# State-space products issued alternately from both partition halves and divided into parts between the k-steps of dense units

## The chip, the cores and the metric

The kernel runs on one core of a Trainium2 chip. The metric is device time in microseconds (us) for one execution. TensorE (PE in the profile) multiplies matrices, VectorE (DVE), ScalarE (ACT) and GpSimd (POOL) do the elementwise work, and SyncE (SP) issues the DMA transfers. Each engine works through its own instruction list in order and waits on semaphores.

## The reference

One layer of a streaming encoder is computed for 1024 prompt positions (with 16 meta tokens ahead of them) and 32 decode positions. An input projection of the normalised rows yields latents for attention, the channels `u` of a state-space mixer and two gates. The state-space mixer is what the change touches:

```
bu = einsum("blgc,gnc->blgn", u, b)              # 64 groups of 16 channels, 64 complex states each
x  = f * bu                                       # complex
h  = associative_scan over positions of lam * h + x
y  = Re(einsum("blgn,gcn->blgc", h, c)) + d * u
s  = gelu(y);  o_b = (s @ w_glu_v) * sigmoid(s @ w_glu_g)
h  = h + (sigmoid(g_a) * o_a + sigmoid(g_b) * o_b) @ w_out
h  = h + relu(rmsnorm(h) @ w_mlp_up)**2 @ w_mlp_down
```

All inputs, weights and outputs are float32.

## The kernel before

All activations lie as 128 channels by 1056 or 1072 positions; a position is (k, t) with t in 0..7, so that the scan over positions is done on 134 blocks of 8 positions, and the products inside a block of 8 are one matrix `M`.

**Dense units.** Each large product is cut into units of 128 output columns. `lin_part` runs over the 8 k-steps of a unit; each k-step has three products (high and low halves of weights and activations in fp32r) times three column chunks, so nine matmuls, 72 in a unit. Their results gather in PSUM tiles `acc` (5 banks in this stage) and are copied out by `finish` on ScalarE. `Weights.get` loads the weights two units ahead and splits them into `wh` (ScalarE, L184) and `wl` (GpSimd, L187) one unit ahead.

**The state-space stage.** It covers about 60 to 470 us of the profile. Eight blocks j of 128 channels (8 groups g of 16) pass through six steps:

- `st0`: loads `U` (the channels of the block), builds the phase table `tb` on GpSimd, and the tables `cl` (tile `clm`) and `wx` (tile `wxt`) on VectorE.
- `st1`: transposes `wx` into `W` (L580), forms the kernel of a block (L590, four quarters of the array's columns), and spreads it by DMA into `M`.
- `st2`: 16 fp32 matmuls (L614) with 64 output rows each, alternately for the lower and the upper 64 columns of the array, give the inputs of the scan in tile `sp`; ScalarE copies them to `xs` (L620 to L622), and VectorE does the scan: `A`, `Bt` (L634 to L637), two scans (L640), two products (L642, L643) and `hb` (L646, L647), the states. All of it needs `tb`.
- `st3`: for each of 8 groups one fp32 matmul with `M` and 128 rows (L662), then two with `cl` and `hb` on 64 rows (L664). Even groups have their states in partitions 0 to 63, odd groups in 64 to 127. Every fp32 matmul stands in the trace as two MATMUL records. ScalarE copies the sums out (L668).
- `st4`, `st5`: GELU on ScalarE, VectorE and GpSimd.

The tiles `sp` of st1, st2 and st3 share three PSUM banks (pool `sps`). `tb`, `xs`, `hb`, `W` and some others have one buffer each, so block j+1 begins `tb` when block j no longer reads it.

**Order.** `START` places the blocks at slots 2, 4, 7, 9, 12, 15, 17 and 20; step d of block j is emitted in slot START[j]+d (st3 has d = 4), and a slot holds all steps due in it, whole, and then one dense unit. The framework turns the emission order into priorities: on each engine the first instruction in emission order that its model of time holds to be ready comes next, and the order so found is fixed before the kernel runs. So slots 6, 11 and 19 hold st3 of one block and st2 of another, slots 8, 13, 16 and 21 st3 and st1, and slot 24 st3 alone. Blocks 0, 2 and 5 are followed by the next block after two slots, the others after three.

After the stage come two more dense units, the GLU units (from about 533 us), attention, the output projections and the MLP.

Of the kernel before, what the change touches and what calls it, by code (L numbers as in the profile page):

```python
# [10 lines left out]
F32 = mybir.dt.float32  # L11
# [3 lines left out]
AF = mybir.ActivationFunctionType  # L15
# [17 lines left out]
KQ = 132  # L33
NQT = T * KQ
CH = [(0, 358), (358, 358), (716, 356)]
CQ = [(0, 352), (352, 352), (704, 352)]
# [86 lines left out]
GQ = [(t0 * KQ, nt * KQ) for t0, nt in G3]  # L123
# [34 lines left out]
def tile_layer(ctx: ExitStack, tc: tile.TileContext, a: dict, o: list, dbg=None):  # L158
    nc = tc.nc
# [77 lines left out]
    w_units = [("u", m) for m in range(8)]  # L237
# [4 lines left out]
    for kind, m in w_units:  # L242
        w0, M = (m * 128, 128 if m < 5 else 64) if kind == "z" else (NQ + 1024 * "uab".index(kind) + m * 128, 128)
# [15 lines left out]
            units += ups(q + 1, range(1, GK))  # L259
    ws = Weights(units)  # L260

    def lin_part(ps, wh, wl, xh, xl, ks, kt, M, chunks):
        for k in ks:
            for p, (w, x) in enumerate(((wh, xh), (wh, xl), (wl, xh))):
                for (c0, n), pt in zip(chunks, ps):
                    nc.tensor.matmul(  # L266
                        pt[:M, :n], lhsT=w[:, k, :], rhs=x(k, c0, n),
                        start=(k == 0 and p == 0), stop=(k == kt - 1 and p == 2),
                    )
        return [(c0, n, pt[:M, :n]) for (c0, n), pt in zip(chunks, ps)]  # L270

    def lin(pool, tag, wh, wl, xh, xl, kt, M=128, chunks=CQ):
        ps = [pool.tile([128, 512], F32, tag=tag, name=tag) for _ in chunks]
        return lin_part(ps, wh, wl, xh, xl, range(kt), kt, M, chunks)

    def rsqrt(pool, v, shape, tag, cap=None):
        R, n = shape
# [22 lines left out]
    gps = ges.enter_context(tc.tile_pool(reuse_waits="tile", name="gps", bufs=5, space=PSUM))  # L300
    with tc.tile_pool(reuse_waits="tile", name="s5", bufs=1) as sp, tc.tile_pool(reuse_waits="tile", name="sps", bufs=3, space=PSUM) as sps:
        xh = xnp.tile([128, 8, NT], F32R, name="xh")
        xl = xnp.tile([128, 8, NT], F32R, name="xl")
        xfull = [lambda k, c0, n, x=x: x[:, k, c0:c0 + n] for x in (xh, xl)]
        xout = [lambda k, c0, n, x=x: x[:, k].rearrange("p (t c) -> p t c", t=T)[:, c0 // KQ:(c0 + n) // KQ, 0:KQ]
                for x in (xh, xl)]

        def finish(kind, m, M, outs, st):
            for c0, n, ps in outs:
                if kind in "ab":  # L310
                    nc.scalar.activation(st[:M, c0:c0 + n], ps, AF.Tanh, scale=0.5)  # L311
                else:
                    nc.scalar.activation(st[:M, c0:c0 + n], ps, AF.Copy)
# [2 lines left out]

        stage = [lambda: sp.tile([128, NT], F32, tag="gst", name="gst", bufs=2)]

        def run_unit(kind, m):
            wh, wl = ws.get()  # L320
            M = 64 if (kind, m) == ("z", 5) else 128
            st = stage[0]()
            if kind == "u" or (kind == "z" and m > 2):
                finish(kind, m, M, lin(gps, "acc", wh, wl, *xfull, 8, M, CH), st)
                nc.sync.dma_start(dst_d[kind][m][:M], st[:M])
            else:
                finish(kind, m, M, lin(gps, "acc", wh, wl, *xout, 8, M, GQ), st)
# [82 lines left out]
        with ExitStack() as _:  # L410
# [102 lines left out]
            for q, nme in enumerate(("ssm_c_re", "ssm_c_im")):  # L513
                cl = sp.tile([128, 4, 2, 64], F32, tag="clt", name="cl")
# [59 lines left out]
            def st1(j):  # L574
                cl, wx = hold[j]["cl"], hold[j]["wx"]
                W = sp.tile([128, 2, 4, 128], F32, tag="W", name="W")
                for q in range(2):
                    pp = sps.tile([128, 4, 128], F32, tag="sp", name="sp")
                    for g in range(4):
                        nc.tensor.transpose(pp[:, g], wx[:, q, g].rearrange("p a b -> p (a b)"), ident)  # L580
                    nc.scalar.activation(W[:, q], pp, AF.Copy)

                for g2 in range(2):
                    hs = slice(64 * g2, 64 * g2 + 64)
                    for q in range(2):
                        V.tensor_copy(bd[hs, q, :, g2, :], bbar[hs, q, 4 * j:4 * j + 4])
                pk = sps.tile([128, 512], F32, tag="sp", name="sp")
                for g in range(4):
                    for q in range(2):
                        nc.tensor.matmul(  # L590
                            pk[32 * g:32 * g + 32, 0:128],
                            lhsT=bd[:, q, g].rearrange("p a b -> p (a b)"),
                            rhs=cl[:, q, g, 0:8].rearrange("p a b -> p (a b)"),
                            start=(q == 0), stop=(q == 1), tile_position=(0, 32 * g),
                        )
                V.tensor_copy(ext[:, 7:15].rearrange("p a b -> p (a b)"), pk[:, 0:128])
                V.scalar_tensor_tensor(ext[:, 7], m16, dd[:, j:j + 1], ext[:, 7], op0=ALU.mult, op1=ALU.add)
                nc.sync.dma_start(ext_d[j], ext.rearrange("p a b -> p (a b)"))
                M = sp.tile([128, 8, 128], F32, tag="M", name="M", bufs=2)
                src = ext_d[j].rearrange("(g c) x -> c g x", c=16)  # L600
                for s in range(T):
                    nc.sync.dma_start(M[16 * s:16 * s + 16], src[:, :, 16 * (7 - s):16 * (7 - s) + 128])
                hold[j].update(W=W, M=M)

            def st2(j):
                gs = slice(4 * j, 4 * j + 4)
# [3 lines left out]
                for g in range(4):  # L610
                    px = sps.tile([128, 512], F32, tag="sp", name="sp")
                    for q in range(2):
                        for g2 in range(2):
                            nc.tensor.matmul(  # L614
                                px[64 * g2:64 * g2 + 64, KC * q:KC * q + KC],
                                lhsT=W[:, q, g, 64 * g2:64 * g2 + 64], rhs=U[:, 2 * g + g2],
                                start=True, stop=True, tile_position=(0, 64 * g2),
                            )
                    pv = px[:, :2 * KC].rearrange("p (q k) -> p q k", q=2)
                    nc.scalar.activation(xs[:, :, g, 3:131], pv[:, :, 0:128], AF.Copy)  # L620
                    nc.scalar.activation(xs[:, :, g, 132:136], pv[:, :, 128:132], AF.Copy)
                    nc.scalar.activation(xs[:, :, g, 1:3], pv[:, :, 132:134], AF.Copy)  # L622
                V.tensor_copy(xs[:, 0, :, 131:132], str_[:, gs][:, :, None])
                V.tensor_copy(xs[:, 1, :, 131:132], sti[:, gs][:, :, None])
                fl = lambda t: t.rearrange("p q a b -> p q (a b)")
# [27 lines left out]
            def st3(j):  # L653
                hj = hold.pop(j)
                U, M, cl, hb = hj["U"], hj["M"], hj["cl"], hj["hb"]
                Y = sp.tile([128, 8, KQ], F32, tag="Y", name="Y", bufs=3)
                for gs in ((0, 2, 4), (1, 3, 5), (6,), (7,)):
                    py = sps.tile([128, 512], F32, tag="sp", name="sp")
                    for e, g in enumerate(gs):
                        c = slice(e * KQ, (e + 1) * KQ)  # L660
                        hs = slice(64 * (g % 2), 64 * (g % 2) + 64)
                        nc.tensor.matmul(py[:, c], lhsT=M[:, g], rhs=U[:, g, 0:KQ], start=True, stop=False)  # L662
                        for q in range(2):
                            nc.tensor.matmul(  # L664
                                py[:, c], lhsT=cl[hs, q, g // 2, 1:9].rearrange("p a b -> p (a b)"),
                                rhs=hb[hs, q, g // 2], start=False, stop=(q == 1),
                            )
                    nc.scalar.activation(  # L668
                        Y[:, gs[0]:gs[-1] + 1:2], py[:, :len(gs) * KQ].rearrange("p (g k) -> p g k", k=KQ), AF.Copy
                    )  # L670
# [884 lines left out]
```

## Time and profile before

| | us |
|---|---|
| median of three runs | 2105.84 (2103.2 to 2112.06) |
| the profiled execution | 2111.11 |
| its span, first to last instruction | 2109.3 |
| PE busy in the span | 2044.5 |
| state-space stage (60 to 470 us): length | 410 |

A matmul record's end is modelled and overlaps the next record, so costs on PE are read from the starts of successive records. "PEclk" is the granted TensorE clock as a share of 2.4 GHz; 0.50 is 1.2 GHz. In the profile's timeline a row gives start, length, engine, line, operation, tiles, shape and the count of instructions merged in it, and in brackets the idle time before it and what ended it.

### The profile page before, as it was taken

What the parts mean: (1) busy time and instruction counts of PE and PEld (TensorE: products, weight loads), DVE (VectorE), ACT (ScalarE), POOL (GpSimd) and SP (SyncE); (2) the same over time, 40 slices, a digit from 0 to 9 for tenths busy, and PEclk for the clock granted to TensorE, in tenths of its full rate; (3) what the DMA queues carried; (4) which work ended last, traced back from release to release, by engine and by line L of the source; (5) the groups of instructions that cost most, each with busy time, mean ns of one, the idle gap of its engine ahead of it and who ended that gap; (6) DMA issues with size and microseconds to landing.
All of it is one profiled execution on the core that took longest, in us unless ns stands there. A gap on an engine that the chain in (4) does not pass through costs nothing.

```text
span 2109.3 us, 34104 instructions
## 1 busy us (share of the span) xinstructions
PE 2044.5 (97%) x12939; PEld 1945.5 (92%) x12939; DVE 1120.0 (53%) x3063; ACT 727.7 (35%) x1736; POOL 695.7 (33%) x924
## 2 busy tenths in 40 slices
PE   4999999999999999999999999999999999999999
PEld 4989989999999878788888899999999999999999
DVE  7968766522766488888886544432322223232222
ACT  4223222223333367567656223231212212121222
POOL 3576666721222243323345112112121222212121
PEclk9989989999999999999999999999999999999999
DMA  6344334435444101111113534512111111211113
GB/s 151 103 120 123 122 115 127 121 108 172 147 125 140 54 12 25 19 22 22 22 20 90 167 118 131 180 31 61 31 55 43 48 54 32 60 31 55 44 42 103
DMA packets 256319, 171.22 MB, mean 81 GB/s; under 512 B 63255, under 2 KB 239468, under 8 KB 256156
## 3 DMA queue, kind: packets, MB, share of 16 engines
q1 hardware_dynamic: 256012, 168.53, 27.4%
q8 instruction: 102, 1.67, 0.3%
q14 instruction: 61, 0.50, 0.1%
q10 hardware_dynamic: 144, 0.52, 0.1%
HBM read 124.60 MB, written 44.41 MB: 80 GB/s over the span
## 4 chain that ended last, share of the span: by engine, by line
PE 85%; DVE 9%; DMA 2%; ACT 2%; issue 1%; POOL 1%; SPq 0%; ACTq 0%; DVEq 0%; POOLq 0%
PE acc L266 42%; PE pj L266 22%; PE po L1253 3%; PE pj L1024 3%; PE sp L664 2%; PE pj L1084 2%; PE pt L1228 1%; PE sp L662 1%; PE Sp L1171 1%; PE Sp L1163 1%; PE Sp L1164 1%; PE Sp L1166 1%; PE Sp L1165 1%; PE pj L1130 1%; PE sp L614 1%
## 5 line engine op out<-in xcount | busy, mean ns | idle before, releaser
L187 POOL TENSOR_TENSOR wl<-raw,wh 128x1024 fp32r<-128x1024 f32 (+2 forms) x166 | 341.9, 2060 | 933.0 <-ACT wh L184 923.1
L184 ACT ACTIVATE wh<-raw 128x1024 fp32r<-128x1024 f32 (+2 forms) x166 | 148.7, 896 | 817.3 <-PE acc L266 370.9
L266 PE MATMUL acc<-xl,wh 128*128 128x264 f32 (+3 forms) x736 | 178.6, 327 | 9.3 <-DVE xl L187 9.3
L266 PE MATMUL acc<-xh,wh 128*128 128x264 f32 (+6 forms) x736 | 182.3, 332 | 0.5 <-ACT gst L311 0.5
L266 PE MATMUL acc<-xh,wl 128*128 128x264 f32 (+3 forms) x736 | 176.1, 326 | 0.0
L266 PEld LDWEIGHTS acc<-xl,wh 128*128 128x128 f32 (+1 forms) x736 | 128.0, 190 | 11.2 <-DVE xl L187 9.6
L266 PEld LDWEIGHTS acc<-xh,wh 128*128 128x128 f32 (+1 forms) x736 | 128.0, 191 | 7.0 <-issue 3.7
L266 PEld LDWEIGHTS acc<-xh,wl 128*128 128x128 f32 (+1 forms) x736 | 128.0, 189 | 1.5 <-issue 0.8
L1480 DVE TENSOR_TENSOR yacc<-pj,yacc 128x352 f32<-128x352 f32 x96 | 44.5, 518 | 139.4 <-PE pj L266 139.4
L1480 DVE TENSOR_TENSOR yacc<-acc,yacc 128x352 f32<-128x352 f32 (+1 forms) x96 | 44.6, 519 | 113.0 <-PE acc L266 113.0
L187 DVE TENSOR_TENSOR al<-t,ah 128x352 fp32r<-128x352 f32 x96 | 64.7, 700 | 71.6 <-ACT ah L184 71.6
L266 PE MATMUL acc<-sh,wh 128*128 128x352 f32 x384 | 93.1, 325 | 0.6 <-DVE st L948 0.4
L266 PE MATMUL acc<-sl,wh 128*128 128x352 f32 x384 | 93.6, 324 | 0.0
L266 PE MATMUL acc<-sh,wl 128*128 128x352 f32 x384 | 93.0, 324 | 0.0
L1462 DVE SCALAR_TENSOR_TENSOR t<-acc,rstd 128x352 f32<-128x352 f32 x48 | 23.5, 519 | 117.9 <-PE acc L266 117.8
L266 PE MATMUL acc<-ah,wl 128*128 128x352 f32 (+1 forms) x384 | 85.2, 324 | 0.0
L266 PE MATMUL pj<-al,wh 128*128 128x352 f32 x384 | 84.6, 324 | 0.0
L266 PE MATMUL pj<-ah,wh 128*128 128x352 f32 x384 | 84.3, 323 | 0.0
L266 PE MATMUL acc<-al,wh 128*128 128x352 f32 (+1 forms) x384 | 84.1, 323 | 0.0
L266 PE MATMUL acc<-ah,wh 128*128 128x352 f32 (+1 forms) x384 | 84.0, 323 | 0.0
L266 PE MATMUL pj<-ah,wl 128*128 128x352 f32 x384 | 84.0, 323 | 0.0
L266 PE MATMUL acc<-ha,wh 128*128 128x352 f32 x360 | 77.5, 323 | 4.1 <-ACT mh__14015 L184 4.1
(466 smaller groups left out, 5457.0 us busy)
## 6 DMA issues: line engine op xcount, KB each, us to landing
raw<-in_w_mlp_up_dram SPq DMA_DIRECT2D x32, 512.0 KB
raw<-in_w_mlp_down_dram SPq DMA_DIRECT2D x64, 256.0 KB
raw<-in_w_in_dram SPq DMA_DIRECT2D x29, 512.0 KB
ud<-gst SPq DMA_DIRECT2D x8, 536.0 KB
U<-ud SPq DMA_DIRECT2D x64, 67.0 KB
yd<-Y SPq DMA_DIRECT2D x64, 66.0 KB
yt<-yd SPq DMA_DIRECT2D x8, 528.0 KB
sd<-gw SPq DMA_DIRECT2D x8, 528.0 KB
```

Of the source, the lines that this page charges most:

```text
L184: nc.scalar.activation(hi, src, AF.Copy)
L187: lo_eng.tensor_tensor(lo, src, hi.bitcast(F32), ALU.subtract)
L266: nc.tensor.matmul(pt[:M, :n], lhsT=w[:, k, :], rhs=x(k, c0, n), start=(k == 0 and p == 0), stop=(k == kt - 1 and p == 2),)
L614: nc.tensor.matmul(px[64 * g2:64 * g2 + 64, KC * q:KC * q + KC], lhsT=W[:, q, g, 64 * g2:64 * g2 + 64], rhs=U[:, 2 * g + g2], start=True, ...
L662: nc.tensor.matmul(py[:, c], lhsT=M[:, g], rhs=U[:, g, 0:KQ], start=True, stop=False)
L664: nc.tensor.matmul(py[:, c], lhsT=cl[hs, q, g // 2, 1:9].rearrange("p a b -> p (a b)"), rhs=hb[hs, q, g // 2], start=False, stop=(q == 1),)
L1024: nc.tensor.matmul(ps[:R], lhsT=x[:, c, k0:k0 + R], rhs=w[:, c, :], start=(c == 0 and q == 0), stop=(c == 1 and q == 2))
L1084: nc.tensor.matmul(ps[:R, :384], lhsT=x[:, c, 128 * i:128 * i + R], rhs=w[:, c, :], start=(c == 0 and q == 0), stop=(c == 2 and q == 2))
L1130: nc.tensor.transpose(pt[:, h, z, :R], qt[:, e, h, z], ident[:R, :R])
L1253: nc.tensor.matmul(po[:, :256], lhsT=w, rhs=x, start=st["first"], stop=(last and q == len(grp) - 1))
L1462: nc.vector.scalar_tensor_tensor(t, ps, 0.0, rstd[:, c], op0=ALU.max, op1=ALU.mult)
L1480: nc.vector.tensor_tensor(yacc[:, m, c], ps, yacc[:, m, c], ALU.add)
```

## The change

`st1`, `st2` and `st3` become generators. `st1` is divided after each of its two groups of transposes and after the L590 products, `st2` after each of its four groups of L614, `st3` into four parts of one pair of groups each. A slot collects the generators and hands them to `run_unit`, and `lin_part` advances each of them by one part ahead of each k-step of the dense unit; what is left is emitted after it. `st0`, `st4` and `st5` are emitted whole as before, and all of a slot's plain steps now come before its generators' parts. `Weights.get` and the `gst` tile of the unit now come before the parts.

Inside `st3`, the groups go in pairs (even, odd): first the two products with `M`, then for each of the two components the product of the lower and of the upper half, into two PSUM tiles, one for each half.

```diff
     def lin_part(ps, wh, wl, xh, xl, ks, kt, M, chunks, between=()):
         for k in ks:
+            for g in between:
+                next(g, None)
             for p, (w, x) in enumerate(((wh, xh), (wh, xl), (wl, xh))):
...
-        def run_unit(kind, m):
+        def run_unit(kind, m, between=()):
             wh, wl = ws.get()
             M = 64 if (kind, m) == ("z", 5) else 128
             st = stage[0]()
...
                     nc.scalar.activation(W[:, q], pp, AF.Copy)
+                    yield
...
                             start=(q == 0), stop=(q == 1), tile_position=(0, 32 * g),
                         )
+                yield
...
                     nc.scalar.activation(xs[:, :, g, 1:3], pv[:, :, 132:134], AF.Copy)
+                    yield
...
-                for gs in ((0, 2, 4), (1, 3, 5), (6,), (7,)):
-                    py = sps.tile([128, 512], F32, tag="sp", name="sp")
-                    for e, g in enumerate(gs):
+                for ps_ in ((0, 1, 2), (3,)):
+                    py = [sps.tile([128, 512], F32, tag="sp", name="sp") for _ in range(2)]
+                    for e, pr in enumerate(ps_):
                         c = slice(e * KQ, (e + 1) * KQ)
-                        hs = slice(64 * (g % 2), 64 * (g % 2) + 64)
-                        nc.tensor.matmul(py[:, c], lhsT=M[:, g], rhs=U[:, g, 0:KQ], start=True, stop=False)
+                        for b in range(2):
+                            nc.tensor.matmul(py[b][:, c], lhsT=M[:, 2 * pr + b], rhs=U[:, 2 * pr + b, 0:KQ],
+                                             start=True, stop=False)
                         for q in range(2):
-                            nc.tensor.matmul(
-                                py[:, c], lhsT=cl[hs, q, g // 2, 1:9].rearrange("p a b -> p (a b)"),
-                                rhs=hb[hs, q, g // 2], start=False, stop=(q == 1),
-                            )
...
+                            for b in range(2):
+                                hs = slice(64 * b, 64 * b + 64)
+                                nc.tensor.matmul(
+                                    py[b][:, c], lhsT=cl[hs, q, pr, 1:9].rearrange("p a b -> p (a b)"),
+                                    rhs=hb[hs, q, pr], start=False, stop=(q == 1),
+                                )
+                        yield
+                    for b in range(2):
+                        nc.scalar.activation(
+                            Y[:, 2 * ps_[0] + b:2 * ps_[-1] + b + 1:2],
+                            py[b][:, :len(ps_) * KQ].rearrange("p (g k) -> p g k", k=KQ), AF.Copy
+                        )
...
             while slot <= START[7] + 6:
+                steps = []
                 for j in range(8):
                     for f, d in ((st5, 6), (st4, 5), (st3, 4), (st2, 2), (st1, 1), (st0, 0)):
                         if slot == START[j] + d:
-                            f(j)
+                            steps.append(f(j))
+
+                steps = [s for s in steps if s is not None]
                 if w_units:
-                    run_unit(*w_units.pop(0))
+                    run_unit(*w_units.pop(0), steps)
+                for s in steps:
+                    for _ in s:
+                        pass
```

## Rows read from the trace of the kernel before

**Rows 1.** The page's head and the engines' busy time.

```profile
span 2109.3 us, 34104 instructions
PE 2044.5 (97%) x12939; PEld 1945.5 (92%) x12939; DVE 1120.0 (53%) x3063; ACT 727.7 (35%) x1736; POOL 695.7 (33%) x924
```

**Rows 2.** Busy time by stage: stretch, length, engines, clock, DMA share, GB/s.

```profile
60.00:470.00 410.00, 403.97 (x2606) 374.10 (x2605) 274.31 (x684) 104.63 (x257) 250.86 (x463) 0.96 0.41 121
533.00:1373.00 840.00, 813.57 (x5139) 749.59 (x5138) 583.74 (x1855) 410.44 (x1097) 259.19 (x349) 0.99 0.27 79
```

**Rows 3.** Tile sp: instructions, ns minimum/median/maximum, first and last start.

```profile
L614 PE MATMUL sp<-U,W x256: 277/278/484, 105.6 to 431.8; 128*64 128x134 f32 x128
L664 PE MATMUL sp<-hb,clm x256: 272/273/587, 136.3 to 460.4; 64*128 64x132 f32 x128
L662 PE MATMUL sp<-U,M x128: 273/276/588, 133.3 to 459.7; 128*128 128x132 f32 x128
```

**Rows 4.** Timeline of PE, a stretch of st3 at 2.4 GHz.

```profile
403.23 0.39 PE L662 MATMUL sp<-U,M 128*128 128x132 f32 x2
403.55 0.71 PE L664 MATMUL sp<-hb,clm 64*128 64x132 f32 x4
404.19 0.49 PE L662 MATMUL sp<-U,M 128*128 128x132 f32 x2
...
405.26 0.49 PE L662 MATMUL sp<-U,M 128*128 128x132 f32 x2
```

**Rows 5.** Timeline of PE, products from column halves and quarters, and dense ones.

```profile
105.56 1.59 PE L614 MATMUL sp<-U,W 128*64 128x134 f32 x24
...
110.62 0.33 PE L266 MATMUL acc<-xl,wh 128*128 128x358 f32 x1
110.87 0.68 PE L614 MATMUL sp<-U,W 128*64 128x134 f32 x8
111.48 0.59 PE L266 MATMUL acc<-xl,wh 128*128 128x358 f32 x2
111.91 0.65 PE L266 MATMUL acc<-xh,wl 128*128 128x358 f32 x3
112.40 0.65 PE L266 MATMUL acc<-xh,wh 128*128 128x358 f32 x3
...
415.17 0.67 PE L590 MATMUL sp<-clm,bd 128*32 128x128 f32 x16
```

**Rows 6.** Timeline of PE, st3 of blocks 0, 1 and 3.

```profile
136.28 0.71 PE L664 MATMUL sp<-hb,clm 64*128 64x132 f32 x4 [2.59 <-DVE hb L646]
...
139.89 0.81 PE L662 MATMUL sp<-U,M 128*128 128x132 f32 x2
...
141.80 0.81 PE L662 MATMUL sp<-U,M 128*128 128x132 f32 x2
...
178.94 0.71 PE L664 MATMUL sp<-hb,clm 64*128 64x132 f32 x4 [0.37 <-DVE hb L646]
...
265.40 0.71 PE L664 MATMUL sp<-hb,clm 64*128 64x132 f32 x4 [2.21 <-DVE hb L646]
```

**Rows 7.** Windows of 5 us around the two stretches at 1.2 GHz.

```profile
135.00:140.00 5.00, 3.72 (x17) 2.87 (x17) 1.62 (x7) 0.19 (x2) 4.14 (x18) 0.80 0.50 145
140.00:145.00 5.00, 5.00 (x16) 3.81 (x17) 0.00 (x0) 0.50 (x1) 4.37 (x17) 0.50 0.77 208
...
155.00:160.00 5.00, 5.00 (x44) 4.41 (x41) 4.83 (x24) 2.25 (x13) 0.18 (x1) 0.99 0.58 180
...
265.00:270.00 5.00, 4.60 (x21) 3.63 (x22) 0.59 (x5) 0.50 (x1) 4.06 (x20) 0.78 0.27 108
...
280.00:285.00 5.00, 5.00 (x43) 4.56 (x42) 5.00 (x15) 1.08 (x2) 4.53 (x10) 0.86 0.59 167
```

**Rows 8.** Timeline of POOL and DVE: phase table and state chain of block 1.

```profile
134.36 0.22 POOL L415 TENSOR_TENSOR tt<-tb,ek 128x4 f32<-128x4 f32 x1
...
154.80 0.38 POOL L423 TENSOR_TENSOR tb<-tt 128x12 f32<-128x12 f32 x1
...
159.75 1.29 DVE L634 TENSOR_TENSOR A<-xs,tb 128x1088 f32<-128x1088 f32 x1 [0.17 <-ACT xs L622]
...
178.81 0.17 DVE L647 TENSOR_TENSOR hb<-A,Bt 128x16 f32<-128x16 f32 x1
```

**Rows 9.** Timeline of ACT, evictions of st3 from PSUM.

```profile
406.48 0.50 ACT L668 ACTIVATE Y<-sp 128x396 f32<-128x396 f32 x1 [1.36 <-issue]
```

More of the change, by code (lines that the diff above doesn't have):

```diff
@@ L260, in tile_layer, with lin_part @@
     ws = Weights(units)
-    def lin_part(ps, wh, wl, xh, xl, ks, kt, M, chunks):
+    def lin_part(ps, wh, wl, xh, xl, ks, kt, M, chunks, between=()):
         for k in ks:
+            for g in between:
+                next(g, None)
             for p, (w, x) in enumerate(((wh, xh), (wh, xl), (wl, xh))):
@@ L270, in lin_part, with lin @@
         return [(c0, n, pt[:M, :n]) for (c0, n), pt in zip(chunks, ps)]
-    def lin(pool, tag, wh, wl, xh, xl, kt, M=128, chunks=CQ):
+    def lin(pool, tag, wh, wl, xh, xl, kt, M=128, chunks=CQ, between=()):
         ps = [pool.tile([128, 512], F32, tag=tag, name=tag) for _ in chunks]
-        return lin_part(ps, wh, wl, xh, xl, range(kt), kt, M, chunks)
+        return lin_part(ps, wh, wl, xh, xl, range(kt), kt, M, chunks, between)
     def rsqrt(pool, v, shape, tag, cap=None):
@@ L323, in run_unit @@
             if kind == "u" or (kind == "z" and m > 2):
-                finish(kind, m, M, lin(gps, "acc", wh, wl, *xfull, 8, M, CH), st)
+                finish(kind, m, M, lin(gps, "acc", wh, wl, *xfull, 8, M, CH, between), st)
                 nc.sync.dma_start(dst_d[kind][m][:M], st[:M])
             else:
-                finish(kind, m, M, lin(gps, "acc", wh, wl, *xout, 8, M, GQ), st)
+                finish(kind, m, M, lin(gps, "acc", wh, wl, *xout, 8, M, GQ, between), st)
                 nc.sync.dma_start(dst_d[kind][m][:, :NQT], st[:, :NQT])
@@ L656, in st3 @@
                 Y = sp.tile([128, 8, KQ], F32, tag="Y", name="Y", bufs=3)
-                for gs in ((0, 2, 4), (1, 3, 5), (6,), (7,)):
-                    py = sps.tile([128, 512], F32, tag="sp", name="sp")
-                    for e, g in enumerate(gs):
+                for ps_ in ((0, 1, 2), (3,)):
+                    py = [sps.tile([128, 512], F32, tag="sp", name="sp") for _ in range(2)]
+                    for e, pr in enumerate(ps_):
                         c = slice(e * KQ, (e + 1) * KQ)
-                        hs = slice(64 * (g % 2), 64 * (g % 2) + 64)
-                        nc.tensor.matmul(py[:, c], lhsT=M[:, g], rhs=U[:, g, 0:KQ], start=True, stop=False)
+                        for b in range(2):
+                            nc.tensor.matmul(py[b][:, c], lhsT=M[:, 2 * pr + b], rhs=U[:, 2 * pr + b, 0:KQ],
+                                             start=True, stop=False)
                         for q in range(2):
-                            nc.tensor.matmul(
-                                py[:, c], lhsT=cl[hs, q, g // 2, 1:9].rearrange("p a b -> p (a b)"),
-                                rhs=hb[hs, q, g // 2], start=False, stop=(q == 1),
-                            )
-                    nc.scalar.activation(
-                        Y[:, gs[0]:gs[-1] + 1:2], py[:, :len(gs) * KQ].rearrange("p (g k) -> p g k", k=KQ), AF.Copy
-                    )
+                            for b in range(2):
[10 more added lines that the diff above has]
+                        )
                 for g in range(8):
```

## The prediction

> **What bounds the kernel.** I read the page's busy times first. PE works 2044.5 of 2109.3 us, no other engine more than 53% [rows 1]. Then the stages: the change lies in the state-space stage, and there PE is busy 404 of 410 us with a mean clock of 0.96, while DVE has 274 and POOL 251 [rows 2]. So in this stage a microsecond taken from PE is a microsecond off the span, unless a chain on DVE and POOL becomes later than PE. Third I read the tile that the three changed steps write, to see how many records each has [rows 3]: L664 and L614 256 each, L662 128, so per block 32, 32 and 16. Last I read single stretches of the timeline for what one record costs.
>
> **st3 at full clock.** The first two L662 behind dense work show the streaming step: 0.39 us less the last record's 0.276 leaves 0.112 us from start to start [rows 3, 4]. A group (two L662, four L664) takes 405.26 - 404.19 = 1.07 us, and six steps of 0.112 are only 0.67. The other 0.395 us is lost at the two borders between 128-row and 64-row products: 403.55 comes 0.32 behind 403.23, where two steps are 0.22 [rows 4]. Before, eight groups pay this eight times a block. After, a pair of groups pays it once: four L662, border, eight L664, border to the dense k-step. Dense work to L662 has no border, since those first two records ran at the plain step [rows 4].
>
> The trace of before has no row in which the lower and upper row halves run side by side, because it issues all L664 of one half in a row. So I bound it.
>
> - Lower bound on the gain: no overlap. A pair costs 12 x 0.112 + 0.395 = 1.74 us against 2.13: 0.395 saved, times 32 pairs = 12.6 us.
> - Upper bound: two at a time. The nearest rows are the column halves: 24 L614 in 1.59 us are (1.59 - 0.278)/23 = 0.057 us each, two in 0.114, and the column quarters of L590 are (0.67 - 0.273)/15 = 0.026 each, four in 0.106 [rows 3, 5]. Then a pair costs 4 x 0.112 + 4 x 0.114 + 0.395 = 1.30 us: 0.834 saved, 26.7 us in all.
>
> I take the upper one: the 0.395 us says that the array really is set up in 64-row tiles for L664, and the columns show that the parts of the array run together.
>
> The Trainium skill, "TensorE: Matmul & The Clock Gate", section "What overlaps and what doesn't", says that matmuls start and end strictly in program order. By that rule the two records of one product could not be passed, eight L664 would take five steps (0.56 us) in place of four, and the gain would be 23.3 us. The trace speaks against it for columns: the code issues four L590 records for one quarter before the next quarter's, which in strict order would need 13 steps of 0.106, 1.4 us, and the 16 took 0.67 [rows 5].
>
> **st2 in four pieces.** Between the dense starts 110.62 and 111.91 lie three dense steps (0.164 each, three in 0.49) and one group of eight L614: 1.29 - 0.49 = 0.80 us, of which 8 x 0.057 = 0.46 is streaming and 0.34 is borders [rows 5]. Before, a block's 32 records ran as 24 and 8, two pieces; after, as four: 2 x 0.34 x 8 = 5.4 us more. In the three slots where a st3 part stands right ahead of the st2 part, one border of half of 0.395 falls away for each of four parts: -2.4. I take +3.0, with 0 and 5.4 as ends.
>
> The Trainium skill, "TensorEngine Tiling (Array Packing)", section "Key Properties", says that changing the tiling mode drains the engine. It speaks against dividing products into parts; the rows agree, and their 0.34 and 0.395 us are its price here.
>
> **st1, evictions, weights.** The transposes of st1 are 128x128 like the dense work, and the L590 group stays whole: 0. The evictions stay four in a block, but the fourth pair needs two of three banks back; two evictions of 0.50 us [rows 9] are covered by the k-step between (nine dense steps, 1.47 us). If ScalarE is late by one eviction each time it costs 8 x 0.5 = 4. I take 1. `Weights.get` moves ahead of the parts: its ScalarE and GpSimd splits are for the next unit and come up to one unit sooner; the DMA loads go past the M and Y transfers on SP's queue. PE waits for none of these anywhere in the stage's waits, so 0.
>
> **Waits and the slow clock.** PE stands 2.59 us for `hb` in block 0 and 2.21 in block 3, 0.37 in block 1: 5.2 [rows 6]. After the first two the granted clock falls to 0.50 (1.2 GHz): 0.80 in 135-140, then 0.50 up to 155, 0.99 in 155-160, which makes 17.1 us; and 13.6 us in the second place [rows 7]. A group then takes 141.80 - 139.89 = 1.91 us, 44% of it lost: 7.5 and 6.0 us. So this costs 18.7 us now. The st3 products kept the clock low; it came back only behind a stretch of dense work in both places.
>
> After, dense k-steps stand between the parts, so I expect some 5 us at 1.2 GHz where there were 17, an estimate between nothing and the 13.6: 2.2 us each. The waits don't go. Block 0's `hb` is fixed by the phase table on POOL, not by PE. For block 1 `tb` takes from 134.36 to 155.18 on POOL, and A to `hb` 19.2 us on DVE, with other work in between [rows 8]. `xs` is the later input now (0.17 us of waiting on it), and st2's parts will come some 10 us earlier, beside st3's and not behind them, so A can start when `tb` ends: 4 us sooner. But st3 of block 1 also moves up by what block 0 saved (3.3 us and its slow clock). I count waits of 1.9, 2 and 3.7 us in blocks 0, 1 and 3 (each an estimate from these rows), with 2.2 behind each: 14.2 against 18.7, so -4.5. The ends are -18.7 (no wait left) and 0.
>
> **Sum.** -26.7 + 3.0 + 1.0 - 4.5 = -27.2. The profiled execution took 2111.11 us, 1.8 more than its span and 5.3 more than the median 2105.84. So 2083.9 in its terms, 2079 at the median of the runs shown. Measurement tells about 0.5%, 10.5 us, from no change: faster is below 2095, slower above 2116.
>
> **Rivals.**
>
> 1. The halves don't overlap. For it: no row shows row halves together. Against it: columns do, and each half gets its own PSUM tile. Then -12.6 + 3.0 + 1.0 - 4.5 = -13.1: 2093.
> 2. The chain takes it back. PE arrives 3 us sooner at each block while `tb` (21 us) and A to `hb` (19 us) stay. Blocks 2, 4, 5 and 7 show no wait today and 0, 1 and 3 do [rows 6]. If the clock's loss stays and one or two more blocks come to wait like block 0, 2.6 + 7.5 = 10.1 each, of the 22.7 left only 2.5 to 12.6 remain: 2093 to 2103, mostly no change.
> 3. Slower by the same mechanism at another place and extent: the order is fixed from a model of time that already put L664 of block 0 ahead of its `hb`, and dense work behind it can't pass. Place: the first L664 of each st3; price 10.1 each; it decides from 22.7/10.1 = 2.2 more blocks on, and four more give +17.7: 2124. Against it: dense parts now end a slow stretch sooner, and in the three-slot gaps (blocks 1, 3, 4, 6 to the next) PE gives the chain a whole slot of 12 us more.
> 4. The order does not follow the emission: the framework lets another instruction pass when it holds a part not ready. Then parts sit together as before; the alternation still saves its 26.7, st2 pays nothing, the slow clock stays: 2079 too. It changes the way, not the time.
>
> Later stages could be reordered by the earlier end: attention idles 26 of 840 us on PE [rows 2]; a fifth of that, 5 us either way, is in the range.
>
> **How the numbers follow.** Forecast (with rival 4) 0.64, its own range 2066 to 2090; rival 1 0.15; rival 2 0.13; rival 3 0.08. The range 2064 to 2102 takes in the first two and half of the third: 0.64 x 0.95 + 0.15 x 0.95 + 0.06 = 0.81. Faster: 0.64 + 0.15 x 0.6 + 0.13 x 0.2 = 0.75; slower 0.08 of rival 3; the same 0.17.
>
> **What would show it.** The timeline of an L664 group: eight records in about 0.73 us (four steps and the last record's end, with a border inside), pairs of starts 0.114 us apart; 1.0 us would be rival 1. Four pieces of eight L614 between dense rows. PE's waits for `hb`: around 7 us in three places; over 15 is rival 2 or 3. The clock of 60 to 470: 0.98 or more. The stage's end (L590 of block 7 now at 415.2) some 25 us earlier. I am wrong if the stage shortens and the span doesn't, or if PE waits for `sp` banks behind ScalarE.

## The result and the profile after

The changed kernel took 2089.93 us (median of four runs, 2084.82 to 2092.18) against 2106.88 for the kernel before on the same chip (four runs): a ratio of 0.9909, with a 95% interval of 0.9888 to 0.9929. That is 17 us faster; 2079 was predicted, with a range of 2064 to 2102. The profiled execution took 2089.60 us, 21.5 less than that of before.

The page's head and busy times of after:

```profile
span 2087.6 us, 34124 instructions
PE 2023.0 (97%) x12939; PEld 1922.7 (92%) x12939; DVE 1122.3 (54%) x3063; ACT 726.7 (35%) x1736; POOL 707.0 (34%) x924
```

PE's busy time fell by 21.5 us, as much as the time [rows 1]. Busy time in the state-space stage of after:

```profile
60.00:470.00 410.00, 403.32 (x2729) 371.57 (x2729) 281.07 (x683) 109.15 (x266) 269.01 (x465) 0.99 0.43 126
```

The stretch holds 123 more PE records in the same 410 us, and its mean clock is 0.99 in place of 0.96 [rows 2]. The transposes of `fin`, which end the state-space stage, start at 474.9 us; before at 495.8. From there on the two traces are equally long within 1 us. So the whole gain lies in the stage, as the prediction assumed.

Timeline of PE in after, one whole pair, then a pair that is divided:

```profile
352.70 0.61 PE L669 MATMUL sp<-U,M 128*128 128x132 f32 x4
353.24 0.72 PE L674 MATMUL sp<-hb,clm 64*128 64x132 f32 x8
353.89 0.68 PE L618 MATMUL sp<-U,W 128*64 128x134 f32 x8
...
355.71 0.61 PE L669 MATMUL sp<-U,M 128*128 128x132 f32 x4
356.25 0.49 PE L674 MATMUL sp<-hb,clm 64*128 64x132 f32 x2
356.67 0.40 PE L268 MATMUL acc<-xh,wh 128*128 128x264 f32 x1
356.90 0.28 PE L268 MATMUL acc<-xl,wh 128*128 128x264 f32 x1
357.02 0.28 PE L268 MATMUL acc<-xh,wl 128*128 128x264 f32 x1
357.24 0.71 PE L674 MATMUL sp<-hb,clm 64*128 64x132 f32 x6
357.88 0.45 PE L268 MATMUL acc<-xh,wh 128*128 128x396 f32 x1
```

Eight L674 have a merged length of 0.72 us, where four took 0.71 before [rows 4]: the row halves do run side by side. The second pair is cut between its second and third L674 by three dense records, which costs two more borders: 355.71 to 357.88 are 2.17 us, less three dense steps of 0.12 are 1.81, against 1.30 for a whole pair (below). 11 of the 32 pairs are cut like this, the fourth of a block in seven blocks and the second in four.

Waits of PE from 60 to 470 us in after (what, us in total, times, longest):

```profile
PE sp L582 <- DVE wxt L419: 6.0, 5, 2.3
PE sp L674 <- DVE hb L651: 0.7, 1, 0.7
```

The waits for `hb`, 5.2 us before [rows 6], are nearly gone. In their place the transposes of `st1` wait 6.0 us for `wx`.

A window of 5 us in after with the start of the stage's only stretch at 1.2 GHz (171.0 to 177.8 us), and the timeline there:

```profile
170.00:175.00 5.00, 3.01 (x10) 3.01 (x11) 5.00 (x12) 1.66 (x5) 3.13 (x4) 0.60 0.01 3
```

```profile
171.99 0.48 PE L582 MATMUL sp<-ident,wxt 128*128 128x128 f32 x1 [2.28 <-DVE wxt L419]
172.12 1.01 PE L268 MATMUL acc<-xh,wh 128*128 128x396 f32 x2
```

Before, 30.8 us ran at 1.2 GHz, 17.1 and 13.7 in two stretches behind waits for `hb` [rows 7]; now 6.8 in one, which begins during the longest of the new waits (169.7 to 172.0) and holds dense records.

### The profile page after: what moved, and what is told of

Its sections match the earlier page's. It is cut to its first block, busy times and chain, and to the rows that moved or that the text cites. A ratio compares the mean times of both kernels' runs of the same rounds, so it can differ in the third digit from the quotient of the medians.

```text
span 2087.6 us, 34124 instructions
## 1 busy us (share of the span) xinstructions
PE 2023.0 (97%) x12939; PEld 1922.7 (92%) x12939; DVE 1122.3 (54%) x3063; ACT 726.7 (35%) x1736; POOL 707.0 (34%) x924
## 3 DMA queue, kind: packets, MB, share of 16 engines
q1 hardware_dynamic: 256012, 168.53, 27.9%
## 4 chain that ended last, share of the span: by engine, by line
PE 85%; DVE 10%; DMA 2%; ACT 2%; issue 1%; SPq 0%; ACTq 0%; DVEq 0%
PE acc L268 42%; PE pj L268 22%; PE po L1272 3%; PE pj L1043 3%; PE pj L1103 2%; PE pt L1247 1%; PE sp L674 1%; PE Sp L1190 1%; PE Sp L1182 1%; PE Sp L1183 1%; PE sp L618 1%; PE Sp L1185 1%; PE Sp L1184 1%; DVE clt L417 1%; PE sp L669 1%
## 5 line engine op out<-in xcount | busy, mean ns | idle before, releaser
L187 POOL TENSOR_TENSOR wl<-raw,wh 128x1024 fp32r<-128x1024 f32 (+2 forms) x166 | 337.4, 2033 | 950.7 <-ACT wh L184 915.8
L268 PE MATMUL acc<-xh,wh 128*128 128x264 f32 (+6 forms) x736 | 189.0, 337 | 0.0
L268 PE MATMUL acc<-xl,wh 128*128 128x264 f32 (+4 forms) x736 | 179.8, 326 | 9.3 <-DVE xl L187 9.3
L268 PE MATMUL acc<-xh,wl 128*128 128x264 f32 (+4 forms) x736 | 179.5, 325 | 0.0
L1481 DVE SCALAR_TENSOR_TENSOR t<-acc,rstd 128x352 f32<-128x352 f32 x48 | 23.5, 518 | 117.9 <-PE acc L268 117.8
```

What stands on the lines that cost most here:

```text
L187: lo_eng.tensor_tensor(lo, src, hi.bitcast(F32), ALU.subtract)
L268: nc.tensor.matmul(pt[:M, :n], lhsT=w[:, k, :], rhs=x(k, c0, n), start=(k == 0 and p == 0), stop=(k == kt - 1 and p == 2),)
L1481: nc.vector.scalar_tensor_tensor(t, ps, 0.0, rstd[:, c], op0=ALU.max, op1=ALU.mult)
```

## The experiments

Each ran against the kernel before on the same chip. Executions of one kernel differ by 7 to 18 us, so times are compared by medians, and traces are read for the mechanism. A trace is of one execution, which may lie far from the median: that of alternation alone lies 9 us below, that of div_only 6 us below, and that of late_clm3 10 us above.

The table's columns are: ratio to before with its interval; the own time of the M and hb records (mean step from start to start at 2.4 GHz, without waits, times 128 and 256); all waits of PE from 60 us to the end of the stage; the length at 1.2 GHz in the stage; the start of the `fin` transposes. Times are us.

| kernel | ratio | M + hb | waits | 1.2 GHz | fin |
|---|---|---|---|---|---|
| before | 1 | 67.0 | 6.1 | 30.8 | 495.8 |
| after | 0.9909 [0.9888, 0.9929] | 44.0 | 6.7 | 6.8 | 474.9 |
| alt_only | 0.9977 [0.9962, 0.9991] | 47.0 | 19.8 | 23.8 | 482.6 |
| div_only | 0.9978 [0.9966, 0.9991] | 60.7 | 4.6 | 0 | 487.0 |
| same_half | 1.0005 [0.9993, 1.0017] | 59.9 | 10.0 | 37.4 | 494.4 |
| st3_div | 0.9972 [0.9959, 0.9986] | 44.0 | 23.5 | 27.2 | 489.3 |
| late_alt | 0.9948 [0.9932, 0.9963] | 46.5 | 21.9 | 20.4 | 485.5 |
| alt_clm3 | 0.9993 [0.9979, 1.0006] | 48.0 | 22.2 | 37.6 | 490.9 |
| alt_tb2 | 1.0007 [0.9992, 1.0022] | 46.5 | 28.3 | 41.0 | 498.0 |
| late_clm3 | 0.9928 [0.9903, 0.9954] | 46.5 | 22.8 | 27.2 | 487.1 |
| st3_div_gelu | 0.9932 [0.9915, 0.9949] | 43.8 | 14.5 | 13.6 | 478.2 |
| late_gelu | 0.9931 [0.9910, 0.9952] | 46.5 | 18.5 | 20.4 | 481.1 |
| late_whole | 0.9959 [0.9945, 0.9974] | 39.9 | 27.9 | 30.6 | 486.1 |
| late_gelu_slot | 1.0013 [1.0000, 1.0026] | 40.0 | 35.8 | 34.1 | 496.7 |

### Each half of the change alone, and pairs without the second half

alt_only keeps the pairs of `st3` and emits every step whole, as before. div_only keeps the divided steps with the old order of groups. same_half emits whole steps and pairs two groups of the same half, so that borders are shared as in the change, but all eight hb records of a pair run on one half. st3_div divides `st3` only. The lines are shown against the changed kernel, with cuts.

```diff
 alt_only
-                    run_unit(*w_units.pop(0), steps)
+                    run_unit(*w_units.pop(0))
 div_only (in st3)
+                for gs in ((0, 2, 4), (1, 3, 5), (6,), (7,)):
...
+                        if g in (2, 1, 5, 7):
+                            yield
 same_half (in st3)
+                for par in range(2):
+                    hs = slice(64 * par, 64 * par + 64)
...
+                        gs = [4 * e + 2 * b + par for b in range(2)]
 st3_div (one yield at the end of st1 and of st2; those of st3 stay)
-                    yield
+                yield
```

> st3 goes over its groups in pairs with the two halves alternating, as in the change, but nothing is divided: all steps of a slot stand whole ahead of the dense unit, as before. Theory A (the alternation brings some 23 us in st3, by the halves running side by side and by half the borders; the division takes away the stretches at 1.2 GHz and pays with borders): about 2082 us, with L664's eight records of a pair in pairs of starts 0.11 us apart, and the slow stretches still there in part. Theory B (the gain of the change comes from the division and the clock): 2095 to 2107 us.

> The three steps are divided as in the change, but st3 keeps its old order of groups (three even ones, three odd ones, two single ones), a part ending after every second group. Theory A: the slow clock goes (some 11 us gained), the borders of the parts cost some 12 us and the waits for wxt some 5: 2103 to 2113 us, no gain. Theory B: at most 2095 us.

> Undivided like alt_only, with as few borders, but a pair is two groups of the same half (0 and 2, 4 and 6, then the odd ones), so nothing can run side by side. If the side-by-side halves matter, st3 saves 12.6 us in place of 26.7 and it is some 14 us slower than alt_only (about 2094), with L664 starts 0.112 us apart one by one. If the borders are all that matters, it is as fast as alt_only.

> The change with st1 and st2 undivided (each whole at its first turn, behind st3's first part); st3 alternated and divided. Theory A: the borders that dividing st1 and st2 costs (some 6 us) fall away, the slow clock stays away: 2082 to 2086 us against 2090 of the change. Theory B: as the change, or slower where a slow stretch comes back.

Medians: alt_only 2102.94, div_only 2103.20, same_half 2108.72, st3_div 2103.24; before there 2107.62. Timeline of PE in same_half:

```profile
366.29 0.61 PE L664 MATMUL sp<-U,M 128*128 128x132 f32 x4
366.83 1.17 PE L667 MATMUL sp<-hb,clm 64*128 64x132 f32 x8
```

Eight records on one half take 1.17 us, on both halves 0.72: that the halves overlap is shown, 0.45 us a pair. But alternation alone, with M and hb at 47.0 us in place of 67.0, is only 5 us faster; same_half, with 12.9 us more of own work there, is 5.8 us slower than it and not 14. Waits of PE and of DVE in alt_only, and one of PE's with the work on DVE that it waits for:

```profile
PE sp L667 <- DVE hb L646: 18.6, 4, 6.4
...
DVE clm L417 <- PE sp L667: 59.7, 6, 11.5
```

```profile
263.96 1.25 PE L667 MATMUL sp<-hb,clm 64*128 64x132 f32 x8 [6.40 <-DVE hb L646]
```

```profile
231.52 1.96 DVE L417 TENSOR_TENSOR clm<-clt 128x144 f32<-128x144 f32 x1 [9.28 <-PE sp L667]
...
241.81 1.28 DVE L634 TENSOR_TENSOR A<-xs,tb 128x1088 f32<-128x1088 f32 x1
...
263.82 0.16 DVE L647 TENSOR_TENSOR hb<-A,Bt 128x16 f32<-128x16 f32 x1
```

`hb` of block 3 is ready at 264.0 us, where before it was at 265.4 [rows 6]: PE has 20 us less work over the stage, and the chain to `hb` has gained 1.4 us by block 3. PE comes early, waits 18.6 us in blocks 0, 1, 3 and 6, and the granted clock falls to 0.50 in each of the waits or within 1 us behind it. My first theory, that alternation alone is worth most of the gain, fell. Division alone, at the low end of its theory A, leaves 4.6 us of waits and no stretch at 1.2 GHz, but pays for borders. (That is its trace, with a mean clock of 0.997 over the whole kernel; its other executions had 0.991 to 0.998, so some may hold such a stretch.) st3_div came out as its theory B has it. The two together give 0.9909, below the product of the two alone, 0.9977 x 0.9978 = 0.9955: each makes the other worth more.

### Filling the wait, or shortening the chain

late_alt emits whole pairs, but ahead of k-step 6 of the slot's dense unit, so that dense work stands between M, `hb` and their inputs. alt_clm3 and alt_tb2 take alt_only and give the chain a buffer more, for the tables `cl` (DVE idles 9.28 us for one above) or for the phase table `tb`. late_clm3 is late_alt with the buffer for `cl`.

```diff
 late_alt (no other yield is left in st1, st2, st3)
             def st3(j):
+                for _ in range(6):
+                    yield
 alt_clm3, alt_tb2, late_clm3: room for the buffer
-                hb = sp.tile([128, 2, 4, KQ], F32, tag="hb", name="hb")
+                hb = sp.tile([128, 2, 4, 136], F32, tag="Gs", name="hb")[:, :, :, 0:KQ]
 alt_clm3, late_clm3 (tag "clm")
-                cl = sp.tile(..., bufs=2)
+                cl = sp.tile(..., bufs=3)
 alt_tb2
-                tb = sp.tile([128, 2, 4, 136], F32, tag="tb", name="tb")
+                tb = sp.tile([128, 2, 4, 136], F32, tag="tb", name="tb", bufs=2)
```

> Alternation in whole steps, but the state products of a block are emitted only ahead of k-step 6 of the dense unit of their slot (k-steps 0 to 5 come first). Theory C (the PE work is shorter by some 20 us as the undivided alternation showed, and only the late hb takes it back; dense work ahead of hb fills that wait): waits for hb in the stage under 4 us instead of 18.6, M and hb records as short as there (about 156 and 105 ns), no or one stretch at 1.2 GHz, 2080 to 2088 us. Rival D (the DVE starts the next block's cl only when this block's hb products have read it, so later products make the next hb later by as much): waits for hb stay over 10 us and the time over 2098.

> Undivided alternation with three buffers for cl in place of two (hb takes the buffer of Gs, which is read for the last time just before hb is written, to make room). Theory D (the DVE idles 9 to 11.5 us in each block ahead of its first write of cl, until the hb products two blocks before have read the buffer, and that delay reaches the next hb): these idle times go, waits for hb fall from 18.6 to under 6 us, slow-clock stretches go with them, 2084 to 2092 us. Rival E (the POOL's phase table, one buffer, is what the first product A waits for in blocks 1, 3 and 6): A starts as late as before there, waits for hb stay over 12 us, 2098 to 2104 us.

> Undivided alternation with two buffers for the phase table in place of one (hb takes the buffer of Gs for the room); TensorE's order is the same as without. Theory E: the table of blocks 1, 3 and 6 ends 8 us or more sooner, A follows it, waits for hb fall from 18.6 to under 6 us, 2084 to 2092 us. Theory D (DVE held by cl): A starts as late as before because the DVE is busy with cl, waits for hb over 12 us, 2098 to 2104 us.

> Both: the state products ahead of k-step 6 of their slot's dense unit, and three buffers for cl. Theory C: as the late kernel with two buffers, within 2 us, because dense work hides the chain there already: 2078 to 2086 us. Theory D: 8 us or more below the late kernel with two buffers, no idle time of the DVE ahead of cl, no wait for hb.

Medians: late_alt 2097.07, alt_clm3 2107.0, alt_tb2 2110.09, late_clm3 2092.0; before there 2109.53. Waits of DVE in alt_clm3, then in alt_tb2, and of PE in late_alt and late_clm3:

```profile
DVE wxt L417 <- PE sp L580: 32.6, 3, 11.8
DVE A L634 <- POOL tb L417: 16.3, 2, 14.2
DVE clm L417 <- PE sp L667: 12.6, 2, 8.7
```

```profile
DVE clm L417 <- PE sp L667: 58.9, 6, 12.4
```

```profile
PE sp L582 <- DVE wxt L419: 12.2, 4, 6.5
PE sp L582 <- DVE wxt L425: 9.3, 3, 5.9
```

```profile
PE acc L268 <- ACT gst L313: 16.5, 3, 9.2
```

A third buffer for `cl` cuts the wait for it from 59.7 us (alt_only) to 12.6, but then DVE waits 32.6 for the one buffer of `wx`, which the transposes read, and A 16.3 for the table. A second table leaves the 58.9 us for `cl`, and A of block 3 starts at 252.39, behind `cl` and `wx` on DVE. PE's wait for `hb` stays at 19.8 and 15.9 us: neither D nor E alone is the cause, and both times lie above what either theory gave. That each link alone meets the others is my reading of these waits; more than one buffer at once was not tried. (`hb` shares the buffer of `Gs` in these kernels; DVE waits 0.4 us for it in late_clm3 and not at all in the other two.) Dense work ahead of `hb` does take the wait for `hb` away, all of it, but the transposes wait for `wx` instead: DVE waits 29.6 us for `cl` and 51.8 at A for the table there, with parts of `wx` queued behind. With the buffer for `cl` that wait is gone too, and the evictions of the dense products are late. late_alt came out between its two theories, and late_clm3, 5.1 us below it, between its own. In all four kernels the wait moves on along a ring of in-order queues.

### The queue of ScalarE

In st3_div too dense products waited 16.1 us for evictions. PE, ACT and POOL there, in that order:

```profile
269.13 0.59 PE L268 MATMUL acc<-xh,wh 128*128 128x264 f32 x1 [5.95 <-ACT gst L313]
```

```profile
266.66 1.08 ACT L699 ACTIVATE gw<-gw 128x1056 f32<-128x1056 f32 x1 [16.80 <-POOL gw L694]
...
268.59 1.15 ACT L313 ACTIVATE gst<-acc 128x396 f32<-128x396 f32 x3
```

```profile
264.22 2.41 POOL L694 TENSOR_TENSOR gw<-gw,yt 128x1056 f32<-128x1056 f32 x1
```

ACT's queue stands at the Tanh of GELU for 16.8 us, because POOL's product for it was put inside the phase table. In after, the same product is ahead of the table, and ACT waits 6.13 us:

```profile
250.18 3.38 POOL L695 TENSOR_TENSOR gw<-gw,yt 128x1056 f32<-128x1056 f32 x1 [0.64 <-DVE gw L694]
...
253.58 1.09 ACT L700 ACTIVATE gw<-gw 128x1056 f32<-128x1056 f32 x1 [6.13 <-POOL gw L695]
```

st3_div_gelu and late_gelu (from late_clm3) form the argument of the Tanh in one DVE operation, so that POOL has no part in GELU. late_whole also takes the first three pairs one k-step sooner and the fourth three k-steps after them. late_gelu_slot begins two k-steps sooner still and has `st4` and `st5` of blocks 0 to 6 one slot later.

```diff
 st3_div_gelu, late_gelu, late_whole, late_gelu_slot
-                V.tensor_scalar(w, w, GELU_C * 0.044715, GELU_C, op0=ALU.mult, op1=ALU.add)
-                nc.gpsimd.tensor_tensor(w, w, yt, ALU.mult)
+                V.scalar_tensor_tensor(w, w, 1.0 / 0.044715, yt, op0=ALU.add, op1=ALU.mult)
...
-                nc.scalar.activation(w, w, AF.Tanh)
+                nc.scalar.activation(w, w, AF.Tanh, scale=GELU_C * 0.044715)
 late_whole (late_gelu_slot: 3 in place of 5)
-                for _ in range(6):
+                for _ in range(5):
                     yield
...
                 for ps_ in ((0, 1, 2), (3,)):
+                    for _ in range(3 if ps_ == (3,) else 0):
+                        yield
 late_gelu_slot
-                    for f, d in ((st5, 6), (st4, 5), (st3, 4),
+                    for f, d in ((st5, 6 + (j < 7)), (st4, 5 + (j < 7)), (st3, 4),
```

> The alternated products alone divided, as measured before at 2103, with GELU's cubic argument formed in one VectorE operation ((w + 1/0.044715) times yt, the factor moved into the Tanh's scale) in place of a VectorE scaling and a GpSimd product. Theory F (ScalarE's queue stands at the Tanh, which waits for GpSimd's product, up to 17.9 us; the evictions of acc queue behind it and the dense products wait for them, 16.1 us in the stage): the wait of dense products for gst falls under 4 us, total PE waits from 23 to under 10 us, 2085 to 2092 us. Rival G (each relief meets the next wait, as in the three kernels with another buffer): another wait of 10 us or more takes its place, 2098 to 2104 us.

> The late state products with three buffers for cl (2092 us, PE waits of 22.8 us in the stage, 16.5 of them dense products that wait for ScalarE's evictions), with GELU's argument in one VectorE operation and no GpSimd product. Theory F: the waits for evictions go, no other takes their place, PE waits under 6 us, fewer stretches at 1.2 GHz, 2074 to 2082 us. Rival G: waits stay over 15 us in another place, 2088 to 2094 us.

> As the late kernel with the one-operation GELU, but the first three pairs ahead of k-step 5 and the fourth pair three k-steps later, when the evictions of the first three are done, so that TensorE's order holds all 32 pairs whole (in the late kernel the fourth pair of each block stands as M, two hb, 17 dense, M, two hb). Theory S (a whole pair costs 1.30 us, as the trace of the late kernel shows three in four times, and the split fourth one 2.14): M and hb records together fall from 46.5 to about 42 us, 3 to 5 us below the late kernel with the one-operation GELU. Rival: the split pair is paid in its own borders only and the extra stretch of dense work between costs as much: within 1.5 us of it.

> As the late kernel with whole pairs, but the pairs begin two k-steps sooner (the first three ahead of k-step 3, the fourth three k-steps later; hb was ready 9 to 11 us ahead of its use there) and the two GELU steps of blocks 0 to 6 come one slot later, so that ScalarE's Square, which waited up to 16.1 us for the load of yt with the evictions of acc behind it, comes after that load. Theory H (that queue is what held the dense products back for 21.9 us): the waits for evictions fall under 5 us, M and hb stay near 40 us, dense records at 166 to 167 ns, 2072 to 2080 us. Rival G (the next wait in line takes it again): waits of 15 us or more in the stage, 2090 to 2100 us.

Medians: st3_div_gelu 2091.99, late_gelu 2093.81, late_whole 2099.14, with 2106.97 before; late_gelu_slot 2109.16 with 2107.02. For st3_div theory F held: the 16.1 us of waits for evictions went to nothing and the ratio from 0.9972 to 0.9932, intervals apart. Of what was freed, 7.1 us came back as waits for `hb` (13.3 in place of 6.2). For the late kernel F failed. Waits of PE and ACT in late_gelu, then of ACT in late_whole:

```profile
PE acc L268 <- ACT gst L313: 12.5, 4, 6.6
...
ACT gw L691 <- issue: 33.7, 3, 14.0
...
ACT gw L691 <- DMA yt<-yd: 28.0, 4, 7.5
```

```profile
ACT gw L693 <- DMA yt<-yd: 67.9, 6, 16.1
```

12.5 of 16.5 us stay, and so does the time. Ahead of the two longest of these four waits of PE, 6.6 and 3.7 us, ACT in late_gelu stands at GELU's Square, for 14.0 and 12.1 us, and the evictions come behind it, the Tanh and a weight split; the profile puts 28.0 us of its waits at Square down to the load of `yt`, the products' own result on its way through DRAM, and 33.7 to nothing that it shows. In late_whole 67.9 us, the longest 16.1, are waits for `yt`: I read it that later products make it later. But putting GELU a slot later did not help: the waits for `yt` were still 62.7 us, the longest 18.7, so theory H fell as I built it, and 17.3 us of waits for ACT's copies to `xs` came on top.

late_whole as a whole came out 5.3 us above late_gelu, where its theory S had 3 to 5 below. But it settles the size of a pair. Timeline of PE in late_alt, the fourth pair of a block, and in late_whole, all four:

```profile
244.51 0.49 PE L668 MATMUL sp<-U,M 128*128 128x132 f32 x2
244.94 0.71 PE L673 MATMUL sp<-hb,clm 64*128 64x132 f32 x4
245.58 0.76 PE L268 MATMUL acc<-xh,wh 128*128 128x396 f32 x3
...
248.51 0.39 PE L668 MATMUL sp<-U,M 128*128 128x132 f32 x2
248.82 0.71 PE L673 MATMUL sp<-hb,clm 64*128 64x132 f32 x4
249.47 0.39 PE L268 MATMUL acc<-xh,wl 128*128 128x264 f32 x1
```

```profile
240.60 0.72 PE L675 MATMUL sp<-hb,clm 64*128 64x132 f32 x8
241.25 0.72 PE L670 MATMUL sp<-U,M 128*128 128x132 f32 x4
241.90 0.72 PE L675 MATMUL sp<-hb,clm 64*128 64x132 f32 x8
...
248.35 0.61 PE L670 MATMUL sp<-U,M 128*128 128x132 f32 x4
248.90 0.72 PE L675 MATMUL sp<-hb,clm 64*128 64x132 f32 x8
```

A whole pair takes 241.90 - 240.60 = 1.30 us. A fourth pair cut in the middle takes 1.07 + 0.96 = 2.03, nearly what two groups took before the change: it stands so because its two tiles need two of three banks back, and the order fixed ahead puts dense work into the gap.

No kernel here beats the change's ratio of 0.9909; late_clm3, late_gelu and st3_div_gelu come within 0.0023 of it, with intervals that overlap its own.

## Why the prediction was right, point by point

**The bound.** Right: a microsecond of PE in the stage was a microsecond of the span, as long as no other queue was later.

**st3, -26.7.** The mechanism and the price of a pair were right: 1.30 us was predicted and 1.30 measured, and with all 32 pairs whole M and hb fall from 67.0 to 39.9, by 27.1. The term was mis-sized because 11 of the 32 pairs aren't whole in the change: it gave -23.0 in those records (44.0). The prediction saw that the fourth pair needs two banks back and charged it as a possible wait of ScalarE (+1.0). No such wait shows; the order pays, by cutting pairs.

The Trainium skill, "TensorE: Matmul & The Clock Gate", section "Part 3: Packing small matmuls — row/col tiling", under "What overlaps and what doesn't", says that matmuls start and end strictly in program order. Taken record by record, that would have made the gain 23.3 us, by the prediction's estimate; with whole pairs the trace has 27.1, and eight records on both halves last as long as four on one (0.72 and 0.71 us). So if the two records of one product stand together in the program, those of the other half pass them. Whether whole products start and end in order no row here shows, and the sixteen L590 records that the prediction sets against the rule don't show it either: their rows don't say which product a record belongs to.

**Division, +3.0 and 0 for st1.** Mis-sized, the largest error. At 2.4 GHz the mean step of the `st2` records rose from 66.8 to 83.1 ns (256 records: +4.2 us), of L590 (now L593) from 39.8 to 52.3 (128: +1.6), and of the dense records from 165.9 to 169.9 (1919 and 1916 records: +7.0 in all), because a dense record on either side of a border takes longer: 356.67 to 356.90 and 357.02 to 357.24 above are 0.23 and 0.22 us for one step of 264 columns, 356.90 to 357.02 is 0.12. That is 12.8 us where 3.0 stood. The step that failed is the count of the borders. Their price was not missing the dense neighbours, since the 0.34 us was read between dense starts [rows 5]. But the prediction counted 32 pieces of `st2` after the change, 12 of them right behind a part of `st3`, whole pairs, and whole L590 groups. The trace of after has 37 pieces of `st2`, 6 of them right behind a part of `st3`, 43 of hb records where whole pairs would make 32, and 12 of L590 (9 before). In st3_div, where `st1` and `st2` stay whole, `st2` is at 70.4 ns, L590 at 39.8, and dense at 167.4.

The Trainium skill, "TensorEngine Tiling (Array Packing)", section "Key Properties", says that a change of tiling mode drains the engine. The trace agrees, and its price here falls on both neighbours of a border.

**Waits and the slow clock, -4.5.** The sign was right and the size too small. The trace of before has 6.1 us of waits (5.2 for `hb`) and 13.9 lost at 1.2 GHz (the steps there less the mean step of the same records at 2.4 GHz), that of after 6.7 and 2.9: 9.6 in place of 20.0, so -10.4. Some 5 us at 1.2 GHz were expected behind each of three waits, and 6.8 came in all. The prediction kept 7.6 us of waits for `hb`; 0.7 are left, since the order puts dense work ahead of the products, and the 6.0 us of waits for `wx` were not foreseen. That the `st3` products kept the clock low is not shown: in after the 6.8 us hold dense records behind a wait, and in before, undivided groups of `st3` ran at 2.4 GHz in other blocks [rows 4].

**Sum.** -23.0 + 12.8 - 10.4, and -0.3 for the transposes of `st1` (64 records, from 111.3 to 107.2 ns), make -20.9, as much as the start of the `fin` transposes moved. The forecast of -27.2 was 6.3 too large in the terms of the profile: 12.2 us too little cost (3.7 in `st3` and 9.8 for the division, less the 1.0 for evictions and this 0.3) against 5.9 too little gain from waits and clock. That the time came into the range is in part luck, then: two errors of opposite sign, and 2089.93 lies at the very end of the forecast's own 2066 to 2090. Most of the rest of the 11 us is the level: the profiled execution of before lay 4.2 above its median, and that of after lay on its own.

**The rivals.** Rival 1 (no overlap) is refuted. Rival 2 (the chain takes it back) did not come for the whole change, but it is what alternation alone does: 2102.94 us, inside its 2093 to 2103, with waits for `hb` up from 5.2 to 18.6. Rival 3 is the same mechanism further on; no kernel here is slower clear of the noise, and of those that wait for `hb` alt_tb2 comes closest, at 1.0007. Rival 4 came in part: the order does not follow the emission, and it cuts pairs and moves the products behind dense work, so it changed the time too, which rival 4 ruled out. The prediction treated the division as a cost with a small credit; the runs show that the alternation pays in full only with the products set among dense work: 0.9977 alone, 0.9909 with the division, 0.9928 in late_clm3, undivided, with six k-steps ahead and a third `cl` buffer.

**What stays open.** Why dividing `st1` and `st2` too brings st3_div from 0.9972 to 0.9909 is shown in part: the order on POOL differs, and taking POOL's product out of ACT's queue gives 0.9932. Whether the rest is due to that same order was not separated.

## What to carry to other kernels

When PE is 97% busy, a cheaper PE step is worth no more than the slack of the chain that feeds it: look, block by block, at how long each input has been ready before it is used, ahead of counting the gain. Independent dense work emitted between the dependent products kept PE going here and its clock up for longer (6.8 us at 1.2 GHz in place of 30.8), but each piece in another tiling mode costs two borders and slows the dense record on either side by 0.1 us, so few and whole pieces are best. A buffer added at one link brought nothing to alternation alone (0.9993 and 1.0007 against 0.9977), where in-order queues hold one another in a ring; follow the queue head (here a Tanh, or a Square that waits for a load) that stands ahead of the eviction that is late.

## What was not expected of the hardware

A DVE operation and a POOL operation beside it can hold each other up. Timeline of DVE in alt_only, and of POOL beside it:

```profile
246.86 0.72 DVE L636 TENSOR_TENSOR A<-A,Bt 128x544 f32<-128x544 f32 x1
247.50 2.99 DVE L637 TENSOR_TENSOR A<-A,Bt 128x544 f32<-128x544 f32 x1
```

```profile
247.02 2.88 POOL L687 TENSOR_TENSOR gw<-gw,yt 128x1056 f32<-128x1056 f32 x1 [6.09 <-DVE gw L686]
```

Two DVE operations of one form and size take 0.72 and 2.99 us; the second ends at 250.49, 0.6 us behind the POOL operation. It does not always go this way. In before the same two take 0.72 us each, and the POOL operation beside them takes 3.54, where it takes 2.4 to 2.5 at its shortest:

```profile
164.03 0.72 DVE L637 TENSOR_TENSOR A<-A,Bt 128x544 f32<-128x544 f32 x1
...
163.56 3.54 POOL L682 TENSOR_TENSOR gw<-gw,yt 128x1056 f32<-128x1056 f32 x1 [8.38 <-DVE gw L681]
```

So a POOL operation of 3 us in the stretch of A to `hb` can hold that chain by about 2 us, though the engines share no data there; what decides which of the two waits was not tested.
